# Sliding windows over a batch of images: SyncE loads 22 of the lower half's channels in all eight pairs, in 14 transfers

## The chip, the cores and the metric

The kernel runs on one core of one Trainium2 chip. The metric is the device time of one execution in microseconds; several runs are summarised by their median, lowest and highest. A profile is one execution taken by the hardware profiler; its span, from the first to the last recorded instruction, is a little shorter than the execution's device time.

## The reference

The input is `x`, 16 images of 64 channels of 64 x 64 float32 (16.8 MB). Every 8 x 8 window at stride 4 is copied out, 15 x 15 windows for each image and channel (59.0 MB). Nothing is computed; all of it is moving data.

```python
n_h = (h - window_size) // stride + 1
n_w = (w - window_size) // stride + 1
result = np.zeros((batch, n_h, n_w, c, window_size, window_size), dtype=np.float32)
for i in range(n_h):
    for j in range(n_w):
        h_start = i * stride
        w_start = j * stride
        result[:, i, j] = x[:, :, h_start:h_start + window_size, w_start:w_start + window_size].copy()
```

## The kernel before

**The picture in SBUF.** The tile `Lt` holds the whole input. A partition is one (channel half, image, quarter of the rows): partitions 0 to 63 hold channels 0 to 31 (the lower half, `ch` = 0), partitions 64 to 127 channels 32 to 63 (the upper half, `ch` = 1). Each partition holds 32 channels of 16 rows, and one channel of one partition is one run of 1024 floats, 4 KB.

**Loading.** Channels 0 to 7 of each half (`FC` = 8) do not go to `Lt` at once. Eight transfers (line 124; four are issued by ScalarE, the ACT queue, and four by SyncE, the SP queue) put them into the output buffer `GG`, each with 16 partitions by 8 channels (512 KB), and line 141 copies them from there to `Lt` with VectorE and ScalarE. These are called the GG loads below. All other channels, 8 to 31 of each half, go straight into `Lt` by `load` (line 61). One call of `load` takes one (y, q): y is a group of eight images (`NY` = 2 groups), q a quarter of the rows (`HQ` = 4). It writes eight partitions, four apart, by as many channels as it is given. The loop at line 126 goes through the eight (y, q); each is a pair, one load of the lower and one of the upper half:

- pairs 0 to 5 (`HWP` = 6): SyncE loads 20 lower channels (12 to 31), GpSimd (the POOL queue) the four lower channels 8 to 11, and then all 24 upper channels;
- pairs 6 and 7: GpSimd loads 24 lower and 24 upper channels.

So GpSimd issues 16 of these loads and SyncE six. A transfer issued by GpSimd is a software transfer (queue q0 in the profile), one issued by SyncE or ScalarE a hardware transfer (q1 and q10).

**Lanes.** Each DMA signals a semaphore. The eight of the software transfers are taken in turn, and so are the eight of the hardware transfers, which SyncE and ScalarE share. A transfer waits, on its issuing engine, until the transfer that had its semaphore eight before it has landed. These semaphores are called lanes.

**Building and storing.** An output tile is built in one of three buffers of `GG` by copies of VectorE and ScalarE out of `Lt`: `part` (lines 183 to 197) makes tiles of 128 rows of 16 KB, `plain` (204 to 213) and `cross` (215 to 230) tiles of 128 rows of 24 KB. GpSimd then scatters each tile to DRAM by an indirect DMA (line 158); there are 21 of these, and the ten of `cross` leave out 16 of their rows each, by an index out of bounds. Two last tiles are built at line 256 and stored by SyncE (line 257, 64 rows of 24 KB each). The first three tiles are `part(0, ...)`, which needs the loads of y = 0 alone; the following ones need all. The order on each engine is the order of the program: GpSimd has its 16 loads, then 21 stores; SyncE has four GG loads, six loads, two stores.

Of the kernel before, what the change touches and what calls it, by code (L numbers as in the profile page):

```python
# [10 lines left out]
def kernel(  # L11
# [7 lines left out]
    nc = tc.nc  # L19
# [12 lines left out]
    HQ = P // (B * CH)  # L32
    CL = C // CH
# [6 lines left out]
    NY = B // YB  # L40
# [13 lines left out]

    SMALL, HWP = 4, 6

    def load(eng, ch, y, q, c0, c1):
        p0 = ch * HP + y * QP + q  # L60
        eng.dma_start(out=L[p0 : p0 + QP - HQ + 1 : HQ, c0:c1, :, :], in_=x_v[ch, y, q, :, c0:c1, :])  # L61
# [53 lines left out]
    FC = 8  # L115
# [5 lines left out]
    for q in range(HQ):  # L121
        for ch in range(CH):
            s = S[ch][QP + q : QP + q + (B - 1) * HQ + 1 : HQ]
            (nc.scalar, nc.sync)[ch].dma_start(out=s, in_=x_b[ch, q, :, 0:FC, :])

    for y in range(NY):
        for q in range(HQ):
            hw = y * HQ + q < HWP
            if hw:
                load(nc.sync, 0, y, q, FC + SMALL, CL)  # L130
            load(nc.gpsimd, 0, y, q, FC, FC + SMALL if hw else CL)
            load(nc.gpsimd, 1, y, q, FC, CL)

    PC = TC // 2
    first = [(0, ch, c) for ch in range(CH) for c in range(0, FC, PC)]
# [157 lines left out]
```

## Time and profile before

| what | value |
|---|---|
| device time, median of 3 runs (lowest to highest) | 185.93 us (185.83 to 185.98) |
| device time of the profiled execution | 185.73 us |
| its span | 184.0 us |
| VectorE busy | 142.8 us (78% of the span) |
| ScalarE busy | 141.6 us (77%) |
| GpSimd busy | 39.5 us (21%) |
| read from and written to DRAM | 16.78 MB and 62.91 MB, 433 GB/s over the span |

The profile is read in microseconds from the start of the span. "Busy" counts the instructions that work on data; the time in which an instruction only starts a transfer counts for GpSimd alone. For the DMA engines, of which the core has 16, the profile gives their mean busy share in each slice of time and the bytes moved. Beside the page, the trace holds a record of every DMA packet (queue, size, start, duration) and every landing event. A software transfer lands with 16 events, one from each DMA engine; a load issued by SyncE into eight partitions lands with eight events and the others counted at its issue. The packet records do not name their DMA engine.

### The profile page before, as it was taken

How to read it: one execution, taken by the hardware profiler on the slowest of the kernel's cores; microseconds unless marked ns; L12 is line 12 of the kernel's file. 1: busy time of each engine (PE TensorE's matmuls, PEld its weight loads, DVE VectorE, ACT ScalarE, POOL GpSimd, SP SyncE). 2: the span in 40 equal slices, each digit the busy share in tenths (PEclk: the TensorE clock that was granted, in tenths of full speed). 3: DMA queues.
4: the chain of work that ended last, by engine and by line, in shares of the span. 5: the costliest groups of instructions: out<-in, count | busy, mean ns of one | idle time of the engine just before them, and what ended most of it. 6: DMA issues, size and time to landing. Idle time of an engine off the chain costs nothing.

```text
span 184.0 us, 501 instructions
## 1 busy us (share of the span) xinstructions
DVE 142.8 (78%) x183; ACT 141.6 (77%) x82; POOL 39.5 (21%) x42
## 2 busy tenths in 40 slices
DVE  4002999999999949979999599898798869978700
ACT  0002999999999969989899489889787869978700
POOL 7500763033330420230122202211220220220000
DMA  4999999999999999999999999999999999999993
GB/s 150 400 412 409 411 413 410 399 394 443 422 431 440 433 431 447 413 435 444 419 438 438 433 429 433 444 433 428 428 428 433 428 435 433 428 428 428 428 428 134
DMA packets 9828, 75.80 MB, mean 412 GB/s; under 512 B 3072, under 2 KB 3072, under 8 KB 7168
## 3 DMA queue, kind: packets, MB, share of 16 engines
q0 software_dynamic: 7504, 64.50, 83.2%
q1 hardware_dynamic: 1744, 9.18, 12.2%
q10 hardware_dynamic: 576, 2.10, 3.1%
q14 instruction: 4, 0.03, 0.0%
HBM read 16.78 MB, written 62.91 MB: 433 GB/s over the span
## 4 chain that ended last, share of the span: by engine, by line
DMA 68%; DVE 19%; issue 3%; POOL 2%; ACT 2%; ACTq 0%; DVEq 0%; PEldq 0%
DMA out_dram<-GG,idx_lo 26%; DMA out_dram<-GG,idx 21%; DMA Lt<-in_x_dram 14%; DVE GG L192 8%; DMA out_dram<-GG,idx_hi 8%; DVE GG L150 7%; POOL Lt L61 2%; ACT GG L256 2%; DVE GG L229 2%; DVE GG L212 1%; ACTq L288 0%; DVE GG L256 0%; DVEq L150 0%; POOL pi L77 0%; DVEq L212 0%
## 5 line engine op out<-in xcount | busy, mean ns | idle before, releaser
L225 ACT COPY GG<-Lt 64x2048 f32<-64x2048 f32 x30 | 56.9, 1897 | 9.6 <-DMA out_dram<-GG,idx 4.8
L150 DVE STREAM_SHUFFLE GG<-Lt 64x1024 f32<-64x1024 f32 (+1 forms) x35 | 50.6, 1444 | 0.9
L192 DVE COPY GG<-Lt 32x2048 f32<-32x2048 f32 x30 | 36.6, 1219 | 4.4 <-DMA out_dram<-GG,idx 3.4
L192 ACT COPY GG<-Lt 32x2048 f32<-32x2048 f32 x18 | 34.1, 1896 | 2.8 <-DMA out_dram<-GG,idx 2.4
L212 ACT COPY GG<-Lt 64x2048 f32<-64x2048 f32 x15 | 28.3, 1897 | 0.8 <-DMA out_dram<-GG,idx_lo 0.5
L141 DVE COPY Lt<-GG 32x2048 f32<-32x2048 f32 x10 | 11.9, 1236 | 13.8 <-DMA GG<-in_x_dram 13.7
L229 DVE COPY GG<-Lt 64x1024 f32<-64x1024 f32 x30 | 20.5, 683 | 0.6
L61 POOL DMA_DIRECT2D Lt<-in_x_dram x16 | 13.8, 873 | 17.5 <-DMA Lt<-in_x_dram 16.8
L158 POOL DMA_INDIRECT out_dram<-GG,idx_y x6 | 9.5, 1578 | 30.7 <-DVE GG L192 26.3
L141 ACT ACT_TABLE_LOAD x1 | 1.3, 1283 | 17.1 <-DMA GG<-in_x_dram 17.1
L212 DVE COPY GG<-Lt 64x2048 f32<-64x2048 f32 x10 | 12.1, 1221 | 0.3
L256 ACT COPY GG<-Lt 32x768 f32<-32x768 f32 x12 | 10.0, 830 | 1.8 <-DMA out_dram<-GG,idx_hi 1.2
L158 POOL DMA_INDIRECT out_dram<-GG,idx_lo x5 | 4.8, 963 | 30.1 <-DVE GG L229 30.1
L141 ACT COPY Lt<-GG 32x2048 f32<-32x2048 f32 x6 | 11.2, 1894 | 0.1
L256 DVE COPY GG<-Lt 32x1280 f32<-32x1280 f32 x12 | 9.8, 819 | 1.6 <-DMA out_dram<-GG,idx_hi 0.9
L158 POOL DMA_INDIRECT out_dram<-GG,idx x5 | 6.2, 1246 | 19.8 <-ACT GG L212 16.7
L158 POOL DMA_INDIRECT out_dram<-GG,idx_hi x5 | 4.9, 976 | 26.0 <-DVE GG L229 18.0
L150 DVE LOAD_MASK_SELECT GG<-Lt x35 | 0.3, 8 | 8.2 <-DMA out_dram<-GG,idx 3.7
L80 DVE TENSOR_SCALAR tb<-pi 128x1 int32<-128x1 int32 x1 | 0.2, 155 | 1.0 <-POOL pi L77 1.0
L83 DVE TENSOR_SCALAR tb<-tb 128x1 int32<-128x1 int32 x2 | 0.3, 153 | 0.0
L86 DVE TENSOR_TENSOR th<-tc,tq 128x1 int32<-128x1 int32 x2 | 0.3, 152 | 0.0
L77 POOL IOTA pi<- 128x1 int32 x1 | 0.1, 124 | 0.4 <-PEq L288 0.4
(20 smaller groups left out, 2.9 us busy)
## 6 DMA issues: line engine op xcount, KB each, us to landing
Lt<-in_x_dram POOLq DMA_DIRECT2D x10, 768.0 KB, 17.8
Lt<-in_x_dram SPq DMA_DIRECT2D x6, 640.0 KB
out_dram<-GG SPq DMA_DIRECT2D x2, 1536.0 KB, 10.1
GG<-in_x_dram ACTq DMA_DIRECT2D x4, 512.0 KB, 14.3
GG<-in_x_dram SPq DMA_DIRECT2D x4, 512.0 KB, 14.7
Lt<-in_x_dram POOLq DMA_DIRECT2D x6, 128.0 KB, 17.8
out_dram<-GG,idx_y POOLq DMA_INDIRECT x6, 12.1
out_dram<-GG,idx POOLq DMA_INDIRECT x5, 13.5
```

Of the source, the lines that this page charges most:

```text
L61: eng.dma_start(out=L[p0 : p0 + QP - HQ + 1 : HQ, c0:c1, :, :], in_=x_v[ch, y, q, :, c0:c1, :])
L80: nc.vector.tensor_scalar(out=d[:, :], in0=pi[:, :], scalar1=shift, scalar2=mask, op0=ALU.logical_shift_right, op1=ALU.bitwise_and)
L83: nc.vector.tensor_scalar(out=d[:, :], in0=a[:, :], scalar1=float(m), scalar2=None, op0=ALU.mult)
L86: nc.vector.tensor_tensor(out=d[:, :], in0=a[:, :], in1=b[:, :], op=op)
L141: tc.keep_in_program_order(copy(out=L[d, c : c + PC, :, :], in_=S[ch][f, c : c + PC]))
L150: nc.vector.stream_shuffle(out=out, in_=in_, mask=mask)
L158: st = nc.gpsimd.indirect_dma_start(out=rows, out_offset=bass.IndirectOffsetOnAxis(ap=ix[:, 0:1], axis=0), in_=g, in_offset=None, element_ ...
L192: (act if n % 3 == 0 else dve)(out=g[d * QP : (d + 1) * QP, ch], in_=L[f : f + QP, :, s * ST : s * ST + WS, cols],)
L212: (copy or (dve if m else shf))(out=g[d, n], in_=L[f, :, half * ST : half * ST + WS, cols])
L225: act(out=g[lo, n], in_=L[f, :, s * ST : s * ST + WS, cols])
L229: dve(out=g[hi, n, :, 0:ST], in_=L[f, :, (s + 1) * ST : RB, cols])
L256: copy(out=g[d, n, c0:c1], in_=L[f, c0:c1, s * ST : s * ST + WS, cols])
```

## The change

The constants `SMALL, HWP = 4, 6` become `SMALL, SPLIT, MOVE = 2, 6, 4`, and the loop that loads into `Lt` becomes another; `load` itself, the GG loads, the compute and the stores stay as they are.

```diff
-    SMALL, HWP = 4, 6
+    SMALL, SPLIT, MOVE = 2, 6, 4
...
     for y in range(NY):
         for q in range(HQ):
-            hw = y * HQ + q < HWP
-            if hw:
-                load(nc.sync, 0, y, q, FC + SMALL, CL)
-            load(nc.gpsimd, 0, y, q, FC, FC + SMALL if hw else CL)
+            first = y * HQ + q < SPLIT
+            last = y * HQ + q == NY * HQ - 1
+            a, b = FC + SMALL, CL
+            if last:
+                a, b = a + SMALL, b - MOVE
+            mid = (a + b) // 2
+            for c0, c1 in [(a, mid), (mid, b)] if first else [(a, b)]:
+                load(nc.sync, 0, y, q, c0, c1)
+            load(nc.gpsimd, 0, y, q, FC, FC + SMALL)
+            if last:
+                load(nc.gpsimd, 0, y, q, b, CL)
+                load(nc.gpsimd, 0, y, q, FC + SMALL, a)
             load(nc.gpsimd, 1, y, q, FC, CL)
```

After it, who loads which channels of the lower half:

| pair | SyncE | GpSimd, lower half | GpSimd, upper half |
|---|---|---|---|
| 0 to 5 | 10 to 20 and 21 to 31 (two transfers of 11 channels) | 8 and 9 | 24 channels |
| 6 | 10 to 31 (one of 22) | 8 and 9 | 24 channels |
| 7 | 12 to 27 (one of 16) | 8 and 9; then 28 to 31; then 10 and 11 | 24 channels |

SyncE issues 14 loads into `Lt` in place of six and GpSimd 18 in place of 16. The order of the instructions on VectorE and ScalarE is the same as before.

## The prediction

> **What bounds the kernel.** I read the page's slices first, then its queues, the waits, the two issuing queues in order of time, and the last microseconds by windows.
>
> ```profile
> DVE  4002999999999949979999599898798869978700
> ACT  0002999999999969989899489889787869978700
> DMA  4999999999999999999999999999999999999993
> DMA packets 9828, 75.80 MB, mean 412 GB/s; under 512 B 3072, under 2 KB 3072, under 8 KB 7168
> ...
> q0 software_dynamic: 7504, 64.50, 83.2%
> q1 hardware_dynamic: 1744, 9.18, 12.2%
> ```
>
> The DMA engines are full from the second slice to the last but one; VectorE and ScalarE have holes from 66 us on, which end at a store's landing. So the end is set by how much the busiest DMA engine has to do; a transfer that lands earlier brings nothing by itself.
>
> ```profile
> 17.00:37.00 20.00, 19.24 (x17) 19.68 (x11) 8.76 (x8) 1.00 1.04 407
> 37.00:44.00 7.00, 6.88 (x6) 6.90 (x5) 2.63 (x2) 1.00 1.04 409
> ...
> 179.00:180.00 1.00, 0.00 (x0) 0.00 (x0) 0.00 (x0) 1.00 1.32 565
> 180.00:181.00 1.00, 0.00 (x0) 0.00 (x0) 0.00 (x0) 1.00 0.75 320
> 181.00:182.00 1.00, 0.00 (x0) 0.00 (x0) 0.00 (x0) 1.00 0.18 74
> 182.00:183.00 1.00, 0.00 (x0) 0.00 (x0) 0.00 (x0) 1.00 0.00 0
> ```
>
> The last two columns are DMA share and GB/s, by the start of packets. Only three 24 KB packets start after 181 us (74 GB/s x 1 us / 24,576 B): the engines do not finish together. In the packet records eight finish at 180.85 to 181.05 us, seven at 181.65 to 182.02, and one at 182.68; the last landing is at 183.04, and the span ends 0.9 us later. That unevenness is what the change can touch.
>
> **Who is late, and why.** The software loads land with 16 events each. The last two of pair 7 (lower half, then upper half):
>
> ```
> lower: 40.57 to 41.19 (8 events)   44.70 to 45.13 (8 events)
> upper: 44.25 to 44.86 (8 events)   44.91 to 45.33 (8 events)
> ```
>
> Eight engines need 24 packets' time for the upper load (41 to 44.5), the other eight for the lower one: a load into eight partitions runs on eight engines, lower halves on one set (L), upper ones on the other (U). SyncE's loads run on L too: while they last (to 36.5 us), the software loads crawl on that set. L ends the loads at a median of 45.14, U at 44.46: L is 0.68 us late, though both had 64 GG packets and 192 others. The difference is in the 4-byte packets of q0, 2864: 37 transfers x 16 completions, 160 left-out rows, and 2112, exactly one for each 4 KB packet of the software loads. A software load thus gives the eight engines that do not carry it as many fillers as the others have packets. L has 8 x 24 = 192 each, U 6 x 4 + 2 x 24 = 72.
>
> Two spans of U's landings give their price. From the upper load of pair 0 (median 17.62) to that of pair 5 (36.63), 19.01 us, lie 120 packets p and 20 fillers f; from there to pair 7's (44.46), 7.83 us, 48 of each. So p + f = 0.1630, p = 0.1575 us, f = 5.5 ns. L's 120 extra fillers make 0.66 us of the 0.68. The records give a filler 9 ns where several follow each other: f is between 5.5 and 9 ns; I take 5.5, which fits the lag.
>
> The lag stays, as every later store gives each engine the same rows, and the queues never run dry: at the end the landings are 181.17 to 181.40 (eight), 181.97 to 182.38 (seven), 183.04 (one). The spacing inside the later set (0, .04, .14, .17, .17, .39, .41) is that of L at 45 us (0, .04, .12, .14, .32, .33, .41, .42): L is the late set. The straggler is made at 148.35 us, where an 8 KB instruction packet (309 ns) and a store packet behind it (1266 ns in place of 912) cost one engine 0.66 us; it is 183.04 - 182.38 = 0.66 at the end.
>
> **The change, part by part.**
>
> *Four lower channels to U.* In pair 7 GpSimd's software loads are now lower, 28-31, lower, upper. Sets alternate from one software load to the next in the trace, so the second runs on U: L has 188 packets, U 196. L: -4 x 0.1575 = -0.63 us; U: +0.63.
>
> *Fillers.* L gets 8 x 24 + 4 = 196 (+4, +0.02 us). U gets 7 x 2 + 2 + 2 = 18 (-54: -0.30 us at 5.5 ns, -0.49 at 9).
>
> *50 packets of each L engine from q0 to q1* (120 to 170). Between the landings of SyncE's first and last load (18.22, 37.08 medians) L did 112 to 116 packets and 82 fillers in 18.86 us: 0.159 to 0.164 each, against 0.1575. The middle, 0.160, is 2 ns more, part of which may be the fillers. Cost: 0 to +0.15 us; I take +0.06. A gain below 0 would need a hardware packet under 159 ns; their records show 159 at the least.
>
> *Eight more transfers on SP.* 14 issues x 0.68 us (its row) = 9.5 us on an engine that otherwise waits:
>
> ```profile
> 0.74 3.09 SPq L124 DMA_DIRECT2D GG<-in_x_dram  x4
> 4.82 13.21 SPq L61 DMA_DIRECT2D Lt<-in_x_dram  x6
> 168.33 6.11 SPq L257 DMA_DIRECT2D out_dram<-GG  x2
> ```
>
> Each waits for the lane of eight before: loads 1 to 8 for GG loads (last landing 17.87), 9 to 14 for loads 1 to 6. The first six are issued by 14.9 us, 66 packets or 10.5 us of L's work; one of 11 takes L 1.75 us, an issue 0.68. Cover: five or more transfers stand in the ring. Eight more completions of 9 ns are 0.07 us per L engine at most. SP's stores, behind them, go at 168 us. Zero, bounds 0 to 0.07.
> [...] The load stage's share of 1.04, with 128 KB transfers in it, says that they overlap.
>
> *POOL's queue.*
>
> ```profile
> 27.05 1.08 POOL L61 DMA_DIRECT2D Lt<-in_x_dram  x1 [0.17 <-issue]
> 30.98 1.21 POOL L61 DMA_DIRECT2D Lt<-in_x_dram  x1 [2.85 <-DMA Lt<-in_x_dram]
> 36.57 1.75 POOL L158 DMA_INDIRECT out_dram<-GG,idx_y  x1 [4.38 <-DMA Lt<-in_x_dram]
> 42.70 1.83 POOL L158 DMA_INDIRECT out_dram<-GG,idx_y  x1 [4.37 <-DVE GG L192]
> ```
>
> Two more loads of 1.2 us stand ahead of the stores. The 18th waits for the 10th. On L each pair now takes 2 packets and 24 fillers in turn with SyncE's packets, about 26 x 0.16 + 2 x 0.16 = 4.5 us where it took 5.3, so the 10th lands near 33 us (36.0 before) and the 18th is out by 35. Behind it waits the first store, whose tile is ready at 35.5. The first tile starts at 29.50, when SyncE's pair 3 has landed; L has 98 packets ahead of that in place of 96, so up to 0.3 us later, and with it the store. Its rows are not wanted before U's loads end, 44.3: cover 7 us. Later stores are issued at least 1.7 us before the ring is empty (at 81.3 for 83.0); without that cover a late tile would cost what it exceeds. Zero.
>
> **Sum.** L: -0.63 + 0.02 + 0.06 = -0.55 us (-0.63 + 0.02 to -0.39). U: +0.33 (+0.14 to +0.33). The landings become 181.3 to 181.7 on U, 181.4 to 181.8 on L, and the straggler 182.5: it still ends last, whichever set it falls on (181.40 + 0.33 + 0.66 = 182.4 on U). Span 184.0 - 0.55 = 183.45. The profiled execution took 185.73, 0.20 below the median; from the median, 185.93 - 0.55 = 185.38, rounded to 185.4.
>
> **Rivals.**
> *Straggler gone.* POOL and SP have more instructions, so instruction packets may move and no longer hit a late engine near the end. Then the last landing is 181.8 and the time 185.93 - 1.2 = 184.7. For: four such packets, all in different places (49.6, 76.9, 107.3, 148.4 us). Against: VectorE's and ScalarE's streams, the longest, are unchanged. 8%.
> *The relief is lost.* L's lag is set by hardware packets rather than fillers (0.68 / 120 = 5.7 ns each): 50 more cost 0.28 us, and with a few dry ring slots L gains 0.35 at most: 185.6 to 185.9. For: the 18.86 us above allow 1.5 to 6 ns. Against: U's two spans price the filler without any hardware packet. 18%.
> *The upper engines become the bound.* If the late set at the end were U, the packets go to the wrong side: +0.33 with the saved fillers, +0.63 without: 186.3 to 186.6, slower. It decides once U's last landing before was later than 182.7 us (183.04 - 0.33). For: no record names an engine. Against: the spacing, and 0.54 us or more between the sets after the first store (49.9 against 49.36). 8%.
> *L's ring runs dry.* SP's short transfers wait for landings; an issue brings its first packet 1.45 us later (0.74 to 2.19 us at the start). Each empty ring costs L up to 1.5 us, six of them 9: 186.9 to 194. It decides when fewer than 9 packets are queued at a landing; I count 55. 7%. [...]
>
> **How the numbers follow.** My forecast, 185.0 to 185.5 with the straggler on an earlier or later engine of its set, has 59%. Faster by over 0.2% (about what a measurement of this kernel can tell from no change: below 185.56) is 0.59 + 0.08 = 0.67; same 0.18; slower 0.08 + 0.07 = 0.15. A range of 184.8 to 186.0 holds the forecast, the lost relief and a part of the first rival, 0.8, and leaves the slower ones out.
>
> **What would show it.** The page should have 9524 packets and 2768 under 512 B, q0 6736 and q1 2208 packets. In the last loads' landings the sets should end within 0.3 us of each other; at the end, too, with one engine 0.5 to 0.9 us behind. Share 1.03 or more to 44 us says that the rings stay full. A gap on L before 44 us, L still behind by 0.5 us, or the late set being U would make this wrong.

## The result, and the profile after

The changed kernel takes 186.09 us (median; 185.80 to 186.47) where the kernel before took 185.77 us (185.53 to 186.10) in the same comparison. The ratio is 1.0016, with a 95% interval of 1.0010 to 1.0023: 0.3 us slower, where 0.55 us faster was forecast. The interval does not hold 1, so the loss is real, though it is smaller than the 0.2% that the prediction took as no change. The time lies 0.09 us above the top of the range.

The profiled execution took 185.8 us, with a span of 184.0 us, as before. It is the quickest of the kernel's 22 (0.29 us under the median), so it shows the place of the loss better than its size.

The page of the changed kernel: busy tenths of VectorE, ScalarE and the DMA engines in 40 slices, the bytes moved in each slice, the packets, and the two queues that carry the loads into `Lt`.

```profile
DVE  4002997999999959979999598979779779987800
ACT  0002999999999969989899488979979779977900
DMA  4999999999999999999999999999999999999994
GB/s 158 402 413 407 407 412 413 407 354 427 420 442 436 427 422 451 434 420 447 411 440 438 443 429 427 433 433 427 433 433 427 422 429 433 422 427 422 433 438 176
DMA packets 9524, 75.80 MB, mean 412 GB/s; under 512 B 2768, under 2 KB 2768, under 8 KB 6864
...
q0 software_dynamic: 6736, 62.86, 81.0%
q1 hardware_dynamic: 2208, 10.81, 14.5%
```

The packet counts are the four that were forecast. There are 304 small packets fewer: 400 fillers (the 4-byte packets of the prediction) fewer, one for each 4 KB packet that left q0, and 96 completions more. The 400 packets of 4 KB are now in q1, with 64 completions of the eight added transfers. The DMA engines are as full as before. But look at the ninth slice of the GB/s line (36.8 to 41.4 us): 354, while the DMA line above it says 9 there too. So the packets there are slower (297 ns in the mean at 39.96 to 41.0 us, against 160 elsewhere). The windows of the same execution, by columns: window, length, busy time of VectorE, ScalarE and GpSimd, clock, DMA share, GB/s:

```profile
17.00:37.00 20.00, 18.64 (x16) 19.52 (x11) 9.43 (x9) 1.00 1.04 411
37.00:44.00 7.00, 6.87 (x7) 6.90 (x5) 2.62 (x2) 1.00 1.04 365
39.75:41.50 1.75, 1.71 (x3) 1.73 (x2) 0.00 (x0) 1.00 1.10 260
179.00:180.00 1.00, 0.00 (x0) 0.00 (x0) 0.00 (x0) 1.00 0.97 418
180.00:181.00 1.00, 0.00 (x0) 0.00 (x0) 0.00 (x0) 1.00 0.97 418
181.00:182.00 1.00, 0.00 (x0) 0.00 (x0) 0.00 (x0) 1.00 0.41 172
182.00:183.00 1.00, 0.00 (x0) 0.00 (x0) 0.00 (x0) 1.00 0.00 0
```

From 17 to 37 us the rate is a little higher than before (411 against 407 GB/s). From 37 to 44 us it is 365 against 409: 44 GB/s x 7 us = 0.31 MB not moved, which at 410 GB/s is 0.75 us of all engines. The hole is narrow: 260 GB/s from 39.75 to 41.50 us, at a share of 1.10. The kernel before has a shallower one at the same place:

```profile
39.75:41.50 1.75, 1.72 (x2) 1.73 (x2) 0.00 (x0) 1.00 1.07 366
```

Its own slow packets, 33 of 185 ns or more, stand at 36.2 to 37.0 and at 40.3 to 41.1 us and make 2.4 us too much in all, 0.15 us for each engine. Why it has them stays open.

In the last microseconds seven 24 KB packets start after 181 us (172 GB/s x 1 us / 24,576 B) where three did.

What runs at 40 us is in the landings. Software load 16 is the one that the change moved to U: pair 7, channels 28 to 31.

```
software load 16 (4 channels):    41.21 to 42.08 (8 events)   43.18 to 44.48 (8 events)
SyncE's 22 channels of pair 6:    41.64 to 41.95
last software load (24 channels): 45.02 to 46.12 (16 events, no gap between the sets)
```

While U carries its four packets per engine, L carries SyncE's load of pair 6. From 39.96 to 41.0 us the 4 KB packets of both queues take 297 ns in the mean (61 packets), against 160 elsewhere. In the whole load stage after 8 us, 117 packets take 185 ns or more, 12.9 us too much in all: 0.8 us for each of 16 engines.

Both sets end the loads late. The 16 events of the last load lie together, so their order alone does not tell the sets apart. But L also carries SyncE's last load, whose eight events lie 0.20 us ahead of L's events of the last software load where the sets are apart (in the kernel without the move, below). Assigned in this way, L's median is 45.24 us and U's 45.26, where L had 45.14 and U 44.46. So U lost 0.80 us, and L, with four packets fewer, 0.10. The stores' packets show the same: the first of them start at 44.48 us, where they started at 43.78. The end follows: six engines' last packets end at 181.18 to 181.37 us, nine at 181.62 to 182.35, and the straggler's at 182.74; the last landing is at 183.11 (183.04 before).

The transfers of SyncE and GpSimd around the change went as expected (start, duration, engine, line, operation, and in brackets the idle time ahead and what ended it):

```profile
4.84 22.19 SPq L61 DMA_DIRECT2D Lt<-in_x_dram  x14
```

```profile
33.23 0.64 POOL L61 DMA_DIRECT2D Lt<-in_x_dram  x1 [2.01 <-DMA Lt<-in_x_dram]
37.00 1.75 POOL L169 DMA_INDIRECT out_dram<-GG,idx_y  x1 [3.13 <-DMA Lt<-in_x_dram]
43.12 1.83 POOL L169 DMA_INDIRECT out_dram<-GG,idx_y  x1 [4.37 <-DVE GG L203]
```

SyncE issues all 14 loads by 27 us, GpSimd's last load starts at 33.23, and the first store at 37.00 (36.57 before), over seven microseconds before its first packets start (44.48).

### The profile page after: what moved, and what is told of

Its sections match the earlier page's. It is cut to its first block, busy times and chain, and to the rows that moved or that the text cites. A ratio compares the mean times of both kernels' runs of the same rounds, so it can differ in the third digit from the quotient of the medians.

```text
span 184.0 us, 517 instructions
## 1 busy us (share of the span) xinstructions
DVE 142.6 (77%) x183; ACT 141.6 (77%) x82; POOL 41.3 (22%) x44
## 4 chain that ended last, share of the span: by engine, by line
DMA 76%; DVE 11%; POOL 2%; ACT 2%; issue 2%; ACTq 0%; DVEq 0%; PEldq 0%
DMA out_dram<-GG,idx_lo 27%; DMA Lt<-in_x_dram 21%; DMA out_dram<-GG,idx 21%; DMA out_dram<-GG,idx_hi 8%; DVE GG L161 6%; POOL Lt L61 2%; ACT GG L267 2%; DVE GG L240 2%; DVE GG L203 2%; DVE GG L223 1%; ACTq L299 0%; DVEq L223 0%; POOL pi L77 0%; DVEq L161 0%; DVEq L203 0%
## 5 line engine op out<-in xcount | busy, mean ns | idle before, releaser
L61 POOL DMA_DIRECT2D Lt<-in_x_dram x18 | 14.9, 831 | 18.0 <-DMA Lt<-in_x_dram 17.5
L169 POOL DMA_INDIRECT out_dram<-GG,idx_hi x5 | 5.5, 1109 | 26.4 <-DVE GG L240 18.0
```

The costliest lines, as they stand in the source:

```text
L169: st = nc.gpsimd.indirect_dma_start(out=rows, out_offset=bass.IndirectOffsetOnAxis(ap=ix[:, 0:1], axis=0), in_=g, in_offset=None, element_ ...
```

## The experiments

Three theories were tested.

- **A**: an engine's time is that of its own packets. Four packets moved from L to U relieve L by 0.63 us wherever they go; the loss must then come from the other part of the change.
- **B**: the partitions of one half take only eight engines' worth of writing, whoever writes. Moving lower channels to U then relieves nothing: L waits for U's writes instead of making its own.
- **C**: as B, but the limit is on the reading side, in the part of DRAM in which the lower channels lie.

All ratios are to the kernel before in the same comparison, with 95% intervals. A "slow packet" below is a 4 KB packet after 8 us of 185 ns or more; the undisturbed ones take about 160 ns. The kernel before has the 33 named above.

### The change without the move

```diff
             if last:
-                a, b = a + SMALL, b - MOVE
+                a = a + SMALL
...
-            load(nc.gpsimd, 0, y, q, FC, FC + SMALL)
-            if last:
-                load(nc.gpsimd, 0, y, q, b, CL)
-                load(nc.gpsimd, 0, y, q, FC + SMALL, a)
+            load(nc.gpsimd, 0, y, q, FC, a)
```

> The four lower channels 28 to 31 of pair 7 stay on the lower eight DMA engines (L); the rest of the change is kept. Theory A, the forecast's: an engine's own packets count alone. L then has 4 packets more than in the changed kernel, +0.63 us, and ends 0.6 us behind the upper engines (U) at the end of the loads: the time is 0.5 us above the changed kernel's, 186.6, ratio to before 1.0045. Theory B: partitions 0 to 63 can take only eight engines' worth of writing, whichever engines write, so the four channels cost L the same wherever they run and cost U double. L then ends as in the changed kernel, U 0.7 to 1.0 us earlier than there, and the time is that of the changed kernel or up to 0.2 below: ratio to before 1.000 to 1.002. The slow packets at 39.8 to 41.5 us (about 110 packets of 4 KB over 184 ns) are gone by B, and unexplained by A.

Measured: 185.79 us (185.66 to 185.89) against 185.66; 1.0008 (0.9999 to 1.0017). Two slow packets are left, and the hole is gone (the window of 39.75 to 41.50 us of this kernel):

```profile
39.75:41.50 1.75, 1.71 (x3) 1.73 (x2) 0.00 (x0) 1.00 1.03 410
```

SyncE's load of pair 6 lands at a median of 41.04 us, where it took until 41.87 with the move: L lost 0.83 us there, more than the 0.63 that four packets fewer save. SyncE's last load (16 channels with the move, 20 without) shows what is left of the two: a median of 44.83 without the move, 45.03 with it, 0.20 us later. This is B's result. Eight more SP transfers and 50 more packets of each L engine in q1 come to 0.13 us, which the interval can't tell from nothing; L ends the loads at 45.01 (45.14 before), U at 43.89 (44.46 before).

### Eight extra channels on U, of either half

In the kernel of the previous experiment, with the software loads of pair 7 in the order of the change, the place of the moved load is given to a second load of channels that are there already: eight of the upper half, or eight of the lower half. Both are extra work for U, of one size; `half` is 1 in one kernel and 0 in the other.

```diff
-            load(nc.gpsimd, 0, y, q, FC, a)
+            load(nc.gpsimd, 0, y, q, FC, FC + SMALL)
+            if last:
+                load(nc.gpsimd, half, 1, 0, CL - 8, CL)
+                load(nc.gpsimd, 0, y, q, FC + SMALL, a)
```

Upper channels:

> As e1_move0, and U loads eight upper channels (24 to 31) of pair 4 a second time, to the same place, in the slot where the changed kernel has its four moved ones: more work than the reference asks for. A and B agree: U gets 8 packets more per engine, +1.26 us, L nothing; no packet doubles its duration; the time is that of e1_move0 within 0.3 us, since U has had about 0.7 us or more in hand against L and the straggler.

Lower channels:

> As e2_again_up8, with eight lower channels (24 to 31) of pair 4 loaded a second time by U in their place. A: no difference from e2_again_up8, in time and in packets. B: U writes into the partitions that L is writing: for about 2.5 us the packets of both sets take about 300 ns in place of 159 (some 128 of them), L ends 1.26 us later and U 2.5, and the time is about 1.2 us above e1_move0, 187.2.

Measured: upper 185.84 us, 1.0007 (0.9997 to 1.0016), two slow packets; lower 187.20 us, 1.0082 (1.0067 to 1.0098), 182 slow packets, 24 us too much in all. The windows of the two, upper channels first:

```profile
39.75:41.50 1.75, 1.71 (x3) 1.73 (x2) 0.27 (x1) 1.00 1.06 417
```

```profile
39.75:41.50 1.75, 1.71 (x3) 1.73 (x2) 0.15 (x1) 1.00 1.09 239
41.50:43.50 2.00, 1.97 (x2) 1.98 (x2) 0.45 (x1) 1.00 1.01 258
```

The same number of bytes on the same engines at the same place: 417 GB/s when they belong to the upper half, 239 when they belong to the lower. U had room for seven more packets of the eight (it was 1.1 us ahead of L in the kernel without the move); the lower half had none. The difference of the two kernels, 1.36 us, is near eight packets of an L engine (8 x 0.159 = 1.27 us), as if L had carried them. This decides against A.

### The move alone

The kernel before, with the lower software load of pair 7 cut in three so that channels 28 to 31 run on U:

```diff
-            load(nc.gpsimd, 0, y, q, FC, FC + SMALL if hw else CL)
+            if y * HQ + q == NY * HQ - 1:
+                load(nc.gpsimd, 0, y, q, FC, FC + 2)
+                load(nc.gpsimd, 0, y, q, CL - 4, CL)
+                load(nc.gpsimd, 0, y, q, FC + 2, CL - 4)
+            else:
+                load(nc.gpsimd, 0, y, q, FC, FC + SMALL if hw else CL)
```

> The kernel before with one edit: in pair 7 the lower channels go in three software loads, 8 and 9 on L, 28 to 31 on U, 10 to 27 on L. A: L 4 packets less, -0.6 us: 185.2, ratio 0.997. B: L nothing, U +1.26 us by four packets at double time, so that U ends the loads after L: between no change and +0.6 us, ratio 1.000 to 1.003, with slow packets where the moved load runs.

Measured: 185.83 us, 1.0009 (1.0000 to 1.0018), 130 slow packets, of which 14, at 36.2 to 37.1 us, are of the kind that the kernel before has there too; the window:

```profile
39.75:41.50 1.75, 1.72 (x2) 1.75 (x1) 0.96 (x1) 1.00 1.12 254
```

The move gains nothing here either, without any of the change's other parts, and it makes the same hole, deeper than the one of the kernel before (254 against 366 GB/s).

### Reading or writing

B and C are told apart by loads that cross. In the kernel with eight extra channels, U reads lower channels and writes them to upper partitions, or reads upper channels and writes them to lower partitions. `p0` is the first partition written (`dst`), `src` the half read:

```diff
-                load(nc.gpsimd, 1, 1, 0, CL - 8, CL)
+                p0 = dst * HP + QP
+                nc.gpsimd.dma_start(out=L[p0 : p0 + QP - HQ + 1 : HQ, CL - 8 : CL, :, :], in_=x_v[src, 1, 0, :, CL - 8 : CL, :])
```

Lower channels to upper partitions:

> As e2_again_up8, but what U loads into channels 24 to 31 of the upper partitions of pair 4 is read from the lower channels in DRAM (those channels of the result hold other data). Theory B (the writing side: partitions 0 to 63 take eight engines' worth): no slow packets, the time of e2_again_up8, 185.8. Theory C (the reading side: two sets of engines that read lower channels disturb each other in DRAM): the time of e3_again_lo8, 187.2, with 150 packets over 250 ns.

Upper channels to lower partitions:

> The other crossing: U reads upper channels and writes them into the lower partitions of pair 4 (those channels of the result hold other data). B: the time of e3_again_lo8, 187.2, with some 150 packets over 250 ns. C: the time of e2_again_up8, 185.8, and none.

Measured: reading lower, writing upper 185.87 us, 1.0012 (1.0002 to 1.0021), two slow packets; reading upper, writing lower 187.23 us, 1.0091 (1.0076 to 1.0105), 173 slow packets. The windows, in the same order:

```profile
39.75:41.50 1.75, 1.72 (x2) 1.73 (x2) 0.00 (x1) 1.00 1.03 408
```

```profile
39.75:41.50 1.75, 1.71 (x3) 1.73 (x2) 0.13 (x1) 1.00 1.10 237
```

What slows both sets is the half that is written. C falls.

### Which channels are on which set, exchanged

The kernel before, with 0 and 1 exchanged as the half in its three calls of `load`: each half is now written by the other set.

```diff
-                load(nc.sync, 0, y, q, FC + SMALL, CL)
-            load(nc.gpsimd, 0, y, q, FC, FC + SMALL if hw else CL)
-            load(nc.gpsimd, 1, y, q, FC, CL)
+                load(nc.sync, 1, y, q, FC + SMALL, CL)
+            load(nc.gpsimd, 1, y, q, FC, FC + SMALL if hw else CL)
+            load(nc.gpsimd, 0, y, q, FC, CL)
```

> The kernel before with the halves exchanged in every direct load: SyncE and the small software loads fill the upper partitions, the 24-channel ones the lower. L now writes partitions 64 to 127 and U 0 to 63 throughout. B: each half is written by one set at a time, so it costs nothing that an engine writes the other half: ratio to before 0.998 to 1.002, no 4 KB packets over 250 ns in the load stage after 8 us but for a few. If a set of engines is slow in the other half by itself, all packets of the stage are, and the time rises by microseconds.

Measured: 191.23 us, 1.0298 (1.0283 to 1.0312): the expectation missed. Two windows of this kernel:

```profile
5.00:22.00 17.00, 0.00 (x0) 0.00 (x0) 1.92 (x4) 1.00 1.04 294
24.00:30.00 6.00, 5.95 (x6) 5.95 (x4) 4.38 (x4) 1.00 1.03 400
```

Later the crossed loads run at 400 GB/s (164 ns a packet, against 410 GB/s and 160 ns before), so the pairing of sets and halves as such costs a few per cent at most. Most of the loss lies in the first 22 us, where the GG loads run too. They write partitions 32 to 95, and the expectation had left them out. In the kernel before, the reading that fits is that they keep to the same pairing as the direct loads; with the direct loads crossed, two sets write each half at once, and the rate is 294 GB/s (227 ns a packet). That agrees with B, but it was read out of the result and not tried by itself.

### Relief without two sets on one half

One more lower channel and one less upper channel are staged through `GG`, whose loads run on all 16 engines (in the kernel before each lands with 16 events, the first at 4.44 to 4.81 us, where a SyncE load into eight partitions lands with eight). SyncE then loads 21 lower channels of each pair, GpSimd 2 lower and 25 upper ones; no load is moved.

```diff
-    FC = 8
+    FC = (9, 7)
...
-            (nc.scalar, nc.sync)[ch].dma_start(out=s, in_=x_b[ch, q, :, 0:FC, :])
+            (nc.scalar, nc.sync)[ch].dma_start(out=s, in_=x_b[ch, q, :, 0 : FC[ch], :])
...
```

> L is relieved without a second writer in its half: nine lower and seven upper channels go through GG in place of eight and eight (these loads run on all 16 engines), and of the direct loads L has 23 channels a pair, 21 of them by SyncE, and U 25; no moved channels. B: L has 8 packets less per engine, -1.26 us, U 8 more and, against before, 62 fillers less, +0.8 us: U's last landing 182.1 to 182.3, the straggler on L 181.9: time 0.6 to 0.9 us under before, ratio 0.995 to 0.997. A (the forecast's count of each engine's own packets) says the same here. If L's lag is not made in the loads, the ratio stays at 1.000 or above.

Measured: 185.37 us (185.21 to 185.97) against 185.61; 0.9993 (0.9984 to 1.0001). The expected gain, 0.995 to 0.997, is missed: the interval holds 1. L ended its loads 1.3 us earlier, as meant (43.6 to 44.0 us, the last event at 44.51), but eight channels are too many: U, with eight packets more, is now the late set (44.8 to 45.3), and at the end the late group lands at 181.90 to 182.50. The grain of this remedy is eight packets on each side, where the lag to be shared out was 0.68 us, four packets.

### The grain of four, through spare partitions

What U may carry for L has to be written to the upper half first. In three versions, U loads channel 8 of pairs 4 to 7 into unused space of `GG` at partitions 64 to 95, and VectorE copies it from there to the lower half of `Lt`. SyncE's share changes a little with the small lower loads (in the last two versions 20 channels in pairs 0 to 3 and 21 in pairs 4 to 7). The first uses loads of one channel:

```diff
+    def aside(q):
+        p0 = 2 * QP + q
+        nc.gpsimd.dma_start(out=X[p0 : p0 + QP - HQ + 1 : HQ, 0:1, :, :], in_=x_v[0, 1, q, :, FC : FC + 1, :])
...
+    low = [(0, q, c, c + 1) for q in range(HQ) for c in range(FC, FC + SMALL)]
+    low += [(1, q, FC + 1, FC + 1 + SMALL) for q in range(HQ)]
+    for n, l in enumerate(low):
+        load(nc.gpsimd, 0, *l)
+        if n < HQ:
+            aside(n)
+        else:
+            load(nc.gpsimd, 1, (n - HQ) // HQ, (n - HQ) % HQ, FC, CL)
...
+    tc.keep_in_program_order(nc.vector.tensor_copy(out=L[QP : 2 * QP, FC : FC + 1, :, :], in_=X[2 * QP : 3 * QP]))
```

> The change's aim without a second writer in the lower half. Lower channel 8 of pairs 4 to 7 is loaded by U into spare partitions 64 to 95 of GG (four software loads of one channel at the head of the queue, 4 packets per U engine), and VectorE copies it from there to the lower half (one copy of 32x1024, some 0.6 us, before the first tile). Everything else as e1_move0, with the small lower loads cut so that the sets still alternate. B: L has 4 packets less and nobody else in its half: its last landing of the loads 44.2 to 44.6 (e1_move0: 44.9 to 45.2), U 44.2 to 45.0 (43.6 to 44.4), no more than a few packets over 185 ns; at the end L about 0.6 us earlier, the time 185.0 to 185.2 for a before of 185.6 to 185.7: ratio 0.9965 to 0.998. If relief of L's engines or partitions is not what counts, the ratio is that of e1_move0, 1.000 to 1.002.

Measured: 200.35 us, 1.0790 (1.0775 to 1.0804), with 1674 slow packets. The rate from 37 to 44 us:

```profile
37.00:44.00 7.00, 0.00 (x0) 0.00 (x0) 1.17 (x2) 1.00 0.78 248
```

This says nothing on B: the 24-channel loads no longer alternate cleanly, and upper halves land on both sets. The landings look as if a one-channel load did not count in the alternation; that is a guess. The second version has two runs of half a channel in each of these loads, and no lower load under two channels:

```diff
-        nc.gpsimd.dma_start(out=X[p0 : p0 + QP - HQ + 1 : HQ, 0:1, :, :], in_=x_v[0, 1, q, :, FC : FC + 1, :])
+        nc.gpsimd.dma_start(out=X[p0 : p0 + QP - HQ + 1 : HQ, :, :], in_=x_h[1, q, :, FC, :, :])
...
-    low = [(0, q, c, c + 1) for q in range(HQ) for c in range(FC, FC + SMALL)]
-    low += [(1, q, FC + 1, FC + 1 + SMALL) for q in range(HQ)]
+    low = [(0, q, c, c + 2) for q in range(HQ) for c in (FC, FC + 2)] + [(1, q, FC + 1, FC + 3) for q in range(HQ)]
```

> As e9_aside, without loads of a single channel: the four loads into the spare partitions go as two half channels each (2 packets of 2 KB per U engine and load), and every small lower load has two channels, so that the sets should alternate as they do in the changed kernel (e9's did not: its loads of 24 channels landed on SyncE's set in part). Expectation as there. B: L has 4 packets less and is alone in its half: its last landing of the loads 44.2 to 44.6, U 44.2 to 45.0, few packets over 185 ns after 20 us, ratio 0.9965 to 0.998. If the sets still do not alternate, packets of 200 ns and more show it through the load stage and the time is microseconds above.

Measured: 200.34 us, 1.0789 (1.0775 to 1.0804), the same time for another reason. The loads are now in order: two slow packets, and all of the last load lands from 44.2 to 44.9 us. (The two runs of half a channel go as one packet: the trace has 4096 packets of 4 KB, as before, and none of 2 KB.) But the timeline of VectorE and then of GpSimd shows:

```profile
44.56 0.68 DVE L159 COPY Lt<-GG 32x1024 f32<-32x1024 f32 x1 [17.56 <-DMA Lt<-in_x_dram]
```

```profile
52.35 1.74 POOL L176 DMA_INDIRECT out_dram<-GG,idx_y  x1 [19.87 <-ACT GG L230]
```

The 0.68 us copy waited 17.56 us for loads into channels that it does not touch, with all the building of tiles queued behind it on VectorE; the first store came 15.8 us late, with the loads done by then and nothing for the DMA engines to do:

```profile
44.00:52.00 8.00, 7.26 (x7) 7.92 (x5) 0.00 (x0) 1.00 0.01 4
```

The third version declares that the copy need not wait for the lower loads:

```diff
-        eng.dma_start(out=L[p0 : p0 + QP - HQ + 1 : HQ, c0:c1, :, :], in_=x_v[ch, y, q, :, c0:c1, :])
+        ld = eng.dma_start(out=L[p0 : p0 + QP - HQ + 1 : HQ, c0:c1, :, :], in_=x_v[ch, y, q, :, c0:c1, :])
+        if ch == 0:
+            tc.add_to_no_dep_group("lower", ld.ins)
...
+    tc.declare_no_dep(cp.ins, group="lower", reason="no load writes this channel of these partitions")
```

> As e10_aside2, whose copy out of the spare partitions waited until 44.4 us for lower loads that it doesn't touch, and held up the first tile; the copy is declared free of them here (channel 8 of those partitions is written by no load). The loads in e10 ended together on both sets (44.2 to 44.7). B: the same here, first store issued at 37 us as in the other kernels, L about 0.6 us earlier than in e1_move0 to the end: 185.0 to 185.2 for a before of 185.6 to 185.7, ratio 0.9965 to 0.998. If relief of the lower set is not what counts, 1.000 to 1.002.

Measured: 185.13 us (184.86 to 185.29) against 185.57 (185.27 to 185.79); 0.9972 (0.9962 to 0.9981). It is faster than the kernel before and, by the ratios, than the changed one. Its windows, and its first store:

```profile
39.75:41.50 1.75, 1.72 (x2) 1.73 (x2) 0.00 (x0) 1.00 1.04 410
180.00:181.00 1.00, 0.00 (x0) 0.00 (x0) 0.00 (x0) 1.00 0.63 270
181.00:182.00 1.00, 0.00 (x0) 0.00 (x0) 0.00 (x0) 1.00 0.06 25
```

```profile
36.62 1.74 POOL L180 DMA_INDIRECT out_dram<-GG,idx_y  x1 [3.13 <-DMA Lt<-in_x_dram]
```

There is no hole at 40 us, and after 181 us one 24 KB packet starts where three did. The 16 events of the last load lie together again, at 44.20 to 45.59 us; by L's software load just ahead, L's are at 44.20 to 44.57 and one at 45.59 (median 44.39), U's at 44.29 to 44.99 (median 44.59). Against the kernel without the move L ends 0.62 us earlier and U 0.70 later, where four packets of own work are 0.63; in the changed kernel L ended 0.23 later and U 1.37. The last landing of all is at 182.59, 0.45 us earlier than before. The same four packets per engine, taken by the same upper engines, gain when they are written to upper partitions and nothing when they are written to lower ones.

## Why the prediction was wrong

- **What bounds the kernel** was right. The DMA engines are full throughout, before and after; in the kernel with eight extra lower channels the last load lands from 46.38 us on (45.02 in the changed kernel), and it takes 187.20 us. But the loads' end alone does not give the time. In the kernel without the move both sets end the loads earlier than before, L by 0.13 us and U by 0.57, and it is not faster: its straggler lands 0.87 us behind the next engine (183.12 against 182.25) in place of 0.66.
- **Who is late, and why**: L was late, as the gain of the last version (0.9972) bears out. That its fillers make it late fits the counts: in the kernel without the move, 54 fillers fewer on each U engine go with an end of U's loads 0.57 us earlier (43.89 against 44.46), while L, with as many fillers as before, ends 0.13 us from where it did. That would be some 10 ns each. But that kernel also lacks the 33 slow packets of the kernel before, 0.15 us for each engine if they are spread evenly; without them it is 8 ns. The price taken, 5.5 ns, was low in either case; the bounds were 5.5 and 9.
- **Four lower channels to U** ("L: -4 x 0.1575 = -0.63 us; U: +0.63") is the step that failed. It counted an engine's own packets and gave a packet one price wherever it writes. The runs show that writing into the lower half of the partitions has eight engines' worth of rate (205 to 213 GB/s from 40.5 to 41.5 us, half of 410; the upper half was not tried by itself): U's packets stayed with what L was waiting for. With U writing there too, the packets of both sets took about 300 ns in place of 160. L saved 0.63 us of its own packets and lost 0.83 in the shared window.
- By that count the move should be worth nothing rather than a loss. Four packets on each of eight U engines and four at the same time on each L engine, each twice as long, make 64 x 0.159 = 10.2 us too much; 12.9 us were found. The other 2.7 us, 0.17 us for each of the 16 engines if they are spread evenly, are what sharing cost beyond that; L's 0.20 us is of this size. Why it exists is open. The median of the changed kernel against that without the move (1.0016 to 1.0008) would make the move's loss 0.15 us; the intervals of the two overlap.
- **No rival held this.** The one called "The relief is lost" gave 185.6 to 185.9 us and a loss of the gain, but through hardware packets and dry rings. Neither was there: 50 more packets in q1 and eight more transfers cost 0.13 us in the median, with an interval from nothing to 0.3 us (1.0008, 0.9999 to 1.0017), and the load stage's share is 1.04 from 17 to 37 and from 37 to 44 us. "L's ring runs dry" did not happen, and the straggler is still there. "The upper engines become the bound" had U late, but by its own four packets, and 186.3 to 186.6 us; here U ends level with L.
- **Zero-cost steps** were right. SP's eight added issues are hidden (the last is out by 27 us, its data land at 45), and GpSimd's two added loads delay the first store by 0.43 us of the seven that were free.
- **The sign to look for** was half right. The two sets do end the loads within 0.3 us of each other (45.24 and 45.26), as forecast, but because U was slowed to L's time and not because L was relieved. A criterion on the difference of two sets can't tell these apart; one on the landing time of L could.
- **The straggler**: the instruction packets moved to 42.2, 76.7, 106.4 and 149.3 us, and the last of them again meets a lengthened store packet (1267 ns). It ends 0.42 us behind the next engine in place of 0.66. In this execution that hides most of the 0.31 us by which the group ahead of it ends later (182.69 against 182.38), which fits its span, that of before, while the median is 0.3 us up. What the straggler does in the slower executions is not shown.
- **"The lag stays"** holds only roughly. Behind the last instruction packet the last event of a store comes 1.10 us after the one ahead of it (150.42 us; 1.06 at 150.68 after the change), and at the end it is 0.66 (0.42). So the straggler's lag shrinks on the way, and that the 0.66 us at the end equal the delay at 148.35 us looks like a coincidence. What makes it shrink stays open.

One microsecond inside the shared stretch shows what the lower half takes from both sets, in the kernel with eight extra lower channels and then in the one that reads upper and writes lower ones:

```profile
40.50:41.50 1.00, 0.97 (x2) 1.00 (x1) 0.00 (x0) 1.00 1.04 205
```

```profile
40.50:41.50 1.00, 0.97 (x2) 0.98 (x2) 0.00 (x0) 1.00 1.07 213
```

The DMA share of the sixteen engines is full, and they move 205 and 213 GB/s, half of 410. Two sets of eight engines, each on its half, moved 410 GB/s (24 to 30 us of the kernel before).

## What to carry to other kernels

Before work is moved from a late set of DMA engines to an idle one, ask what the late set is waiting for: if it is the side that is written, as here, other engines bring no rate there, and both sets are slowed (from 160 ns for a 4 KB packet to 297). A window in which the DMA share is full and the rate is not (1.10 and 260 GB/s here) is the sign of it; one extra load of equal size, written to either side, tells the two cases apart (417 against 239 GB/s here). The sign alone does not name the cause: the kernel before has it too, weakly (1.07 and 366 GB/s), and there it stays unexplained. When a helper copy is put on an engine that builds the output, look at what it waits for, not at how long it takes: 0.68 us of work cost 15 us.

## What the runs showed of the hardware

- Two sets of eight engines, each writing its own half of the partitions, move 410 GB/s at 160 ns for a 4 KB packet. When both write the lower half, it is 205 to 213 GB/s from 40.5 to 41.5 us, whichever half of the channels the added load reads; in the changed kernel's shared stretch a 4 KB packet takes 297 ns in the mean (61 packets).
- The 4-byte packets of q0 hold one for each 4 KB packet of the software loads (2112 before and 1712 after, as many as the 4 KB packets in q0). That they go to the eight engines that do not carry the load was not shown, as no record names an engine. At 5.5 ns each, the prediction's estimate, L's 120 extra fillers make 0.66 us of the 0.68 by which it is late; the kernel without the move gives an estimate of 8 to 10 ns.
- Fourteen loads of SyncE in place of six, into the same partitions, cost 0.13 us in the median, with an interval from nothing to 0.3 us.
